# TensorE's order written out: attention steps between half chunks, the memory's scale moved to its evictions

## The chip, the cores and the metric

The kernel runs on one core of one Trainium2 chip. The metric is the device time of one execution in microseconds; the time before is 349.41 us, the median of 3 runs (348.76 to 350.09). Everything is computed in 32-bit floats: a projection product is made of three matmuls in the fp32r type (high part by high part, high by low, low by high), for which each weight and each activation is first split into a rounded high part and the remainder.

## The reference, cut to what matters

```
h = rmsnorm(x, norm_w);  proj = h @ w_in           # 256 tokens, 1024 -> 10752 columns
o_a = dilated_mixture(3 groups of q, k, v)          # 8 heads of 64, ALiBi
o_b = moba_attention(q, k, v)                       # 8 heads; 256 tokens: one causal block
kv  = rmsnorm(mem, mem_norm_w) @ w_mem_kv           # 256 memory tokens
o_m = memory_cross_attention(m_q, m_k, m_v)         # 4 heads
p_i = (o_i * silu(gate_i)) @ w_branch_i             # i = a, b, m
merged = sum_i sigmoid(logit_i + b_merge_i) * p_i
out = rmsnorm(x + merged @ w_out, final_norm_w)
```

## The kernel before, in words

All weights stream through as 54 chunks, listed by `_plan` in the order in which they are loaded, split and multiplied. A chunk is 128 x 2048 numbers: 256 columns of a projection with all 1024 rows, or an equal part of a branch or output matrix. Chunks 0 to 5 are q, k, v of branch b (two halves each), 6 to 10 the gates, 11 to 13 the memory's k and v and the query that reads it (Mk, Mv, Mq), 14 to 31 branch a (two halves of the heads, each with three dilation groups of q, k, v), 32 to 49 merge logits (L) and branch matrices (W), 50 to 53 the output matrix.

`load(i + 3)` puts a chunk's load on SP's queue. `split` has ScalarE cast the raw weights to the high part `wh` (3 buffers) and VectorE subtract it for the low part `wl` (2 buffers), in halves, two chunks ahead. TensorE then does 48 matmuls for the chunk, 24 for each half (`mm_feat` with the weights stationary, `mm_tok` with the activations stationary), into one of three PSUM banks `pj`. An eviction by ScalarE or VectorE follows: a gate chunk is read by a tanh and a product `g` (L633, L635), a query or key by `split_q` or `split_k`, which write fp32r high and low parts for the scores.

Attention runs beside the chunks. Each pair of heads is a list of steps: scores and softmax (`scores`: matmuls, then VectorE, ScalarE, VectorE), transposes of the weights through TensorE with a copy by ScalarE (`trans`), and the weighted values with the gate (`pv`). `chain` gives each step a slot, 2 x chunk + half; `pump` issues the steps that are due, between the two halves of a chunk or at its end. Slots of b start at chunk 12, those of m at chunk 16, those of a in the chunks behind each half of its heads. The scale of the memory's norm is computed by `mem_norm` (two squares on ScalarE, a power on POOL), spread over the partitions by one matmul with ones (`spread`) and multiplied into the memory in `mem_split`, ahead of the matmuls.

The order of the instructions on an engine is not the program's: a planner takes, by its own costs, the first instruction in the program's order that is ready when the engine comes free. So an attention step can run chunks earlier than its slot, and its matmuls can lie between those of a projection. Only for the last output chunk is TensorE's order the program's (`tc.manual_schedule`, L683). The order is fixed when the kernel is built; on the chip each engine goes through it and waits where something isn't ready.

Of the kernel before, what the change touches and what calls it, by code (L numbers as in the profile page):

```python
# [7 lines left out]
F32 = mybir.dt.float32  # L8
# [3 lines left out]
ALU = mybir.AluOpType  # L12
PSUM = bass.MemoryType.PSUM

P = 128
# [15 lines left out]
def _plan():  # L31

    out = []
    b0 = 5120
    for i, n in enumerate(ANAMES):
        for hf in range(2):
            out.append(("B" + n, hf, "in", b0 + 512 * i + (256 * hf if i else 0)))
    for hf in range(2):
        out.append(("G", ("b", hf), "in", 6656 + 256 * hf))
    for hf in range(2):  # L40
        out.append(("G", ("a", hf), "in", 4608 + 256 * hf))
    out.append(("G", ("m", 0), "in", 7424))
    out.append(("Mk", 0, "mem", 0))
    out.append(("Mv", 0, "mem", 256))
    out.append(("Mq", 0, "in", 7168))
    for hf in range(2):
        for g in range(3):
            for i, n in enumerate(ANAMES):
                out.append(("A" + n, (hf, g), "in", 1536 * g + 512 * i + 256 * hf))
    for br, off in (("b", 1), ("m", 2), ("a", 0)):  # L50
        for hf in range(2):
            for j in range(2):
                out.append(("L", (br, 2 * hf + j), "in", 7680 + 1024 * off + 256 * (2 * hf + j)))
            out.append(("W", (br, hf), br, 512 * hf))
    for j in range(4):
        out.append(("O", j, "out", 256 * j))
    return out
# [6 lines left out]
def kernel(ctx: ExitStack, tc: tile.TileContext, wts: bass.AP, xT_d: bass.AP, memT_d: bass.AP,  # L64
# [142 lines left out]
        nc.sync.dma_start(memst["T"], memT_d)  # L207

    def mem_norm():
        _, memst["dg"] = stats(memst["nat"], "m")  # L210

    def mem_split(lo, hi):
        if lo == 0:
            memst["h"] = cp.tile([P, KD, S], F32R, tag="xr", name="mh", bufs=2)
            memst["l"] = cp.tile([P, KD, S], F32R, tag="xr", name="ml", bufs=2)
        mt, mh, ml = memst["T"], memst["h"], memst["l"]
        for k in range(lo, hi):
            nc.vector.scalar_tensor_tensor(mt[:, k, :], mt[:, k, :], mnw[:, k:k + 1], rb["m"],
                                           op0=ALU.mult, op1=ALU.mult)
        for k in range(lo, hi, 2):  # L220
            nc.scalar.copy(mh[:, k:k + 2], mt[:, k:k + 2])
            nc.vector.tensor_tensor(ml[:, k:k + 2], mt[:, k:k + 2], mh[:, k:k + 2].bitcast(F32), op=ALU.subtract)


    def rtile(name):
# [318 lines left out]
                                       rb["x"][:, None, :].to_broadcast([P, 2, S]), op0=ALU.mult, op1=ALU.mult)  # L544


    for i, (kind, key, src, col) in enumerate(PLAN):
        if 0 < i < NCH - 3:
            load(i + 3)
        if i == 1:  # L550
# [15 lines left out]
        if i in (7, 11):  # L566
            hf = (i - 7) // 4
            qkv["Bkx", hf] = split_k(qkv["Bk", hf], f"Bk{hf}")
        if i == 7:
            mem_norm()  # L570
        if i in (9, 10):
            mem_split(4 * (i - 9), 4 * (i - 8))
        nat = kind[0] == "B"
        ah, al = (XH, XL) if nat else (HH, HL)
        if src == "mem":
# [2 lines left out]
        if kind in ("W", "O"):  # L578
            pass
        else:  # L580
            if i == 0:
                pss = [pa.tile([P, 512], F32, tag=("s", "pt")[f // 2], name=f"pj0{f}") for f in range(4)]
            elif i > 1:
                ps = pj.tile([P, 512], F32, tag="pj", name=f"pj{i}")
            if i < 2:
                mm_feat_outer(pss, i, XH, XL)
                split(i + 2, 2, 4)
                split(i + 2, 3, 4)
            for n in range(2 if i > 1 else 0):
                if tok:  # L590
                    mm_tok(ps, S * n, i, [a[:, P * n:P * (n + 1)] for a in ah], [a[:, P * n:P * (n + 1)] for a in al])
                else:
                    mm_feat(ps, S * n, i, KD, S, n, ah, al)
                if n == 0:
                    pump(i, 0)
                    if i == 3:
                        rb["x"] = spread(dgx, "x")
                    if i == 8:
                        rb["m"] = spread(memst["dg"], "m")
                    if i + 2 < NCH:  # L600
                        split(i + 2, 1, 2)
# [12 lines left out]
        elif kind in ("Aq", "Ak", "Av", "Mq", "Mk", "Mv"):  # L614
            at = (kind,) + (key if kind[0] == "A" else (0,))
            if kind[1] == "q" and at[-1] == 0:
                qkv[at] = split_q(ps, -SCALE, f"{kind}{i}")
            elif kind[1] == "k" and at[-1] == 0:
                qkv[at] = split_k(ps, f"{kind}{i}")
            elif kind == "Av" and key[1] > 0:  # L620

                hf, g = key
                if g == 1:
                    stacked[hf] = tp.tile([P, 2, 2, S], F32, tag="vs", name=f"vs{hf}")
                for r in range(2):
                    nc.scalar.copy(stacked[hf][64 * (g - 1):64 * g, :, r, :],
                                   ps[64 * r:64 * (r + 1)].rearrange("p (e c) -> p e c", e=2))
            else:
                t = qkv[at] = rtile(f"{kind}{i}")
                nc.scalar.mul(t, ps, -SCALE if kind == "Aq" else 1.0)  # L630
# [5 lines left out]
        elif kind == "L":  # L636
            br, bk = key
            th = ths[br, bk] = tp.tile([P, 512], F32, tag="th", name="thl")
            off = {"a": 0, "b": 8, "m": 16}[br]
            for n in range(2):  # L640
                c = off + 2 * bk + n
                nc.scalar.activation(th[:, S * n:S * (n + 1)], ps[:, S * n:S * (n + 1)], AF.Tanh, bias=hb[:, c:c + 1],
                                     scale=0.5)
        elif kind == "W":
            br, hf = key
            kn = 2 if br == "m" else 4
            oh = [og[br, k][0] for k in range(kn)]
            ol = [og[br, k][1] for k in range(kn)]
            if "t" not in acc:
                acc["t"] = cp.tile([P, 4, 512], F32, tag="xt", name="acc")  # L650
            for j in range(2):
                bk = 2 * hf + j
                ps = pj.tile([P, 512], F32, tag="pj", name=f"pw{i}{j}")
                for n in range(2):
                    mm_feat(ps, S * n, i, kn, 512, 2 * j + n, oh, ol)
                    if j == 1 and n == 0 and i + 2 < NCH:
                        split(i + 2, 1, 2)
                a = acc["t"][:, bk, :]
                if br == "b":
                    nc.vector.scalar_tensor_tensor(a, ths[br, bk], 1.0, ps, op0=ALU.add, op1=ALU.mult)  # L660
                else:
                    tmp = tp.tile([P, 512], F32, tag="mt", name="mt", bufs=1)
                    nc.vector.scalar_tensor_tensor(tmp, ths[br, bk], 1.0, ps, op0=ALU.add, op1=ALU.mult)
                    if br == "m":
                        nc.gpsimd.tensor_tensor(a, a, tmp, op=ALU.add)
                    else:
                        nc.vector.tensor_tensor(a, a, tmp, op=ALU.add)
                        mh = rp.tile([P, 2, S], F32R, tag="r", name=f"mgh{bk}")
                        ml = rp.tile([P, 2, S], F32R, tag="r", name=f"mgl{bk}")
                        nc.scalar.copy(mh.rearrange("p a b -> p (a b)"), a)  # L670
                        nc.vector.tensor_tensor(ml.rearrange("p a b -> p (a b)"), a,
                                                mh.rearrange("p a b -> p (a b)").bitcast(F32), op=ALU.subtract)
                        merged[bk] = (mh, ml)
                if j == 0:
                    pump(i, 0)
        else:
            if key < 2:
                order = [(key, i, 0), (key, i, 1)]
            elif key == 2:
                order = [(key, i, 0)]  # L680
            else:
                order = [(key, i, 0), (key - 1, i - 1, 1), (key, i, 1)]
            with tc.manual_schedule(engines={mybir.EngineType.PE}) if key == 3 else ExitStack():  # L683
                for kc, wi, t in order:
                    out_mm(kc, wi, t)
                    if t == 0 and i + 2 < NCH:
                        split(i + 2, 1, 2)
                    if kc == 3:
                        finish(t)
        if kind == "Bv" and key == 1:  # L690
            chain([pair_steps_b(p) for p in range(4)], 2 * i + 14, 2)
        elif kind == "Mq":
            chain([pair_steps_m(p) for p in range(2)], 2 * i + 6, 2)
        elif kind == "Av" and key[1] == 2:
            chain([pair_steps_a(2 * key[0] + p) for p in range(2)], 2 * i + 2, 4)
        pump(i, 1)
    assert not steps


# [63 lines left out]
```

## Time and profile before

| | |
|---|---|
| median of 3 runs | 349.41 us |
| profiled execution, its own time | 349.35 us |
| span of the profile | 347.6 us |
| TensorE matmuls busy | 338.2 us (97 %), 2924 |
| VectorE busy | 232.7 us (67 %) |
| ScalarE busy | 206.8 us (60 %) |
| mean granted TensorE clock | 0.994 |

The span runs from the first to the last instruction; the execution's own time holds 1.75 us more. A matmul's busy time contains its way through the array, and matmuls overlap, so what one costs is read from the distance between two starts and not from its duration. In the timeline, equal instructions in a row are merged: "x8" is eight of them, and the time beside it runs from the start of the first to the end of the last.

### The profile page before, as it was taken

Reading aid. Unit: us, or ns where it says so; the run is one execution under the profiler, and the core shown is the slowest. Engines: PE = TensorE matmul, PEld = TensorE weight load, DVE = VectorE, ACT = ScalarE, POOL = GpSimd, SP = SyncE. Lnnn points to the kernel's source line nnn. Section 1 sums busy time; section 2 is a strip of 40 time slices with the busy share of each in tenths; the row PEclk is TensorE's granted clock in tenths of the full one; section 3 lists DMA queues with packets and bytes.
Section 4 is the critical chain, followed back from the end, with each engine's and each line's share of the span. In section 5 each row is a group of like instructions: output and inputs, shape, how many; then the busy total and the mean of one; then the engine's idle time right before and its main releaser. Section 6 shows DMA issues by size and latency. Waiting matters only on the chain.

```text
span 347.6 us, 7107 instructions
## 1 busy us (share of the span) xinstructions
PE 338.2 (97%) x2924; PEld 323.6 (93%) x2924; DVE 232.7 (67%) x405; ACT 206.8 (60%) x367; POOL 27.1 (8%) x40
## 2 busy tenths in 40 slices
PE   8989999999999999999999999999999999999992
PEld 5989999999999988999999999999999999999882
DVE  3849999996878863537785444666453747667554
ACT  6767799575858664637856364765643465546322
POOL 2402000100001000000101000010000304000022
PEclk9999999999999999999999999999999999999997
DMA  7998788650475443354443436345235457646003
GB/s 205 317 413 329 252 352 269 238 210 19 143 275 183 138 173 123 121 219 145 128 163 133 186 130 234 124 158 191 75 123 181 135 232 241 243 138 226 0 3 122
DMA packets 12946, 63.33 MB, mean 182 GB/s; under 512 B 1393, under 2 KB 2801, under 8 KB 6641
## 3 DMA queue, kind: packets, MB, share of 16 engines
q1 hardware_dynamic: 12912, 62.88, 51.0%
q8 instruction: 23, 0.38, 0.4%
q14 instruction: 11, 0.08, 0.1%
HBM read 61.82 MB, written 1.05 MB: 181 GB/s over the span
## 4 chain that ended last, share of the span: by engine, by line
PE 90%; DMA 4%; DVE 2%; SPq 2%; ACT 1%; issue 1%; POOL 0%; POOLq 0%; DVEq 0%
PE pj L234 17%; PE pj L237 17%; PE pj L235 17%; PE pj L254 5%; PE pj L256 5%; PE pj L255 5%; PE pt L322 3%; PE pw L234 3%; PE pw L235 3%; PE pw L237 3%; DMA xn<-in_x 3%; PE y L494 2%; PE y L493 2%; PE y L495 2%; DMA wraw<-in_wts 2%; PE oa L389 1%
## 5 line engine op out<-in xcount | busy, mean ns | idle before, releaser
L94 DVE TENSOR_TENSOR wl<-wraw,wh 128x1024 fp32r<-128x1024 f32 (+2 forms) x117 | 129.7, 1145 | 65.7 <-issue 49.2
L93 ACT CAST wh<-wraw 128x1024 fp32r<-128x1024 f32 (+2 forms) x117 | 108.1, 968 | 49.5 <-PE pj L235 32.2
L234 PE MATMUL pj<-hh,wh 128*128 128x256 f32 x480 | 114.9, 281 | 0.7 <-DVE ssq_m L143 0.7
L235 PE MATMUL pj<-hl,wh 128*128 128x256 f32 x480 | 114.2, 279 | 0.2 <-DVE hl L199 0.2
L234 PEld LDWEIGHTS pj<-hh,wh 128*128 128x128 f32 x480 | 90.3, 188 | 1.8 <-PE sb L299 0.8
L235 PEld LDWEIGHTS pj<-hl,wh 128*128 128x128 f32 x480 | 90.4, 188 | 0.8 <-DVE hl L199 0.4
L237 PE MATMUL pj<-hh,wl 128*128 128x256 f32 x480 | 66.3, 279 | 0.0
L237 PEld LDWEIGHTS pj<-hh,wl 128*128 128x128 f32 x480 | 60.0, 188 | 0.0
L254 PE MATMUL pj<-wh,hh 128*128 128x256 f32 x96 | 27.0, 281 | 0.0
L256 PE MATMUL pj<-wh,hl 128*128 128x256 f32 x96 | 26.8, 279 | 0.0
L255 PE MATMUL pj<-wl,hh 128*128 128x256 f32 x96 | 26.6, 277 | 0.0
L314 ACT ACTIVATE u<-u,st 128x384 f32<-128x384 f32 (+2 forms) x32 | 16.9, 529 | 13.1 <-DVE st L308 13.1
L323 ACT COPY ptsb<-pt 128x384 f32<-128x384 f32 (+1 forms) x28 | 13.1, 497 | 10.4 <-PE pt L322 10.3
L254 PEld LDWEIGHTS pj<-wh,hh 128*128 128x128 f32 x96 | 18.0, 188 | 0.5 <-issue 0.4
L256 PEld LDWEIGHTS pj<-wh,hl 128*128 128x128 f32 x96 | 18.0, 188 | 0.4 <-issue 0.4
L255 PEld LDWEIGHTS pj<-wl,hh 128*128 128x128 f32 x96 | 18.0, 188 | 0.0
L356 POOL TENSOR_SCALAR nba<-con 128x512 f32<-128x512 f32 x8 | 5.0, 624 | 143.6 <-DVE st L308 143.2
L316 DVE TENSOR_SCALAR u<-u,st 128x256 f32<-128x256 f32 (+2 forms) x40 | 15.1, 398 | 0.6
L494 PE MATMUL y<-wl,mgh 128*128 128x512 f32 (+1 forms) x40 | 13.9, 348 | 0.0
L493 PE MATMUL y<-wh,mgh 128*128 128x512 f32 (+1 forms) x40 | 13.9, 347 | 0.0
L495 PE MATMUL y<-wh,mgl 128*128 128x512 f32 (+1 forms) x40 | 13.9, 346 | 0.0
L322 PE MATMUL pt<-con,u 128*128 128x128 f32 x88 | 13.0, 274 | 0.0
(195 smaller groups left out, 552.8 us busy)
## 6 DMA issues: line engine op xcount, KB each, us to landing
wraw<-in_wts SPq DMA_DIRECT2D x48, 1024.0 KB, 4.8
wraw<-in_wts SPq DMA_DIRECT2D x15, 256.0 KB, 5.7
xn<-in_x SPq DMA_DIRECT2D x1, 1024.0 KB, 9.0
memT<-in_memT SPq DMA_DIRECT2D x1, 1024.0 KB, 5.2
memn<-in_mem SPq DMA_DIRECT2D x1, 1024.0 KB, 8.0
xres<-in_xr SPq DMA_DIRECT2D x1, 1024.0 KB, 4.7
wraw<-in_wts SPq DMA_DIRECT2D x2, 512.0 KB, 3.2
out<-ysb SPq DMA_DIRECT2D x4, 256.0 KB, 2.0
```

The source lines that it names most:

```text
L93: nc.scalar.copy(whs[i][:, sl], raws[i][:, sl])
L94: lower[i] = nc.vector.tensor_tensor(wls[i][:, sl], raws[i][:, sl], whs[i][:, sl].bitcast(F32), op=ALU.subtract)
L234: nc.tensor.matmul(ps[:, lo:lo + S], wh[:, k, fs], ah[k], start=(k == 0), stop=False)
L235: nc.tensor.matmul(ps[:, lo:lo + S], wh[:, k, fs], al[k], start=False, stop=False)
L237: nc.tensor.matmul(ps[:, lo:lo + S], wl[:, k, fs], ah[k], start=False, stop=(k == kn - 1))
L254: nc.tensor.matmul(ps[:, lo:lo + S], ah[k], wh[:, k, :], start=(k == 0), stop=False)
L255: nc.tensor.matmul(ps[:, lo:lo + S], ah[k], wl[:, k, :], start=False, stop=False)
L256: nc.tensor.matmul(ps[:, lo:lo + S], al[k], wh[:, k, :], start=False, stop=(k == KD - 1))
L322: nc.tensor.transpose(ps[:, P * j:P * (j + 1)], u[:, P * c:P * (c + 1)], ident)
L493: nc.tensor.matmul(y[t, n][:, 0:w], ht, wh[:, k, cs], start=(kc == 0 and k == 0), stop=False)
L494: nc.tensor.matmul(y[t, n][:, 0:w], ht, wl[:, k, cs], start=False, stop=False)
L495: nc.tensor.matmul(y[t, n][:, 0:w], lt, wh[:, k, cs], start=False, stop=(kc == 3 and k == 1))
```

## The change

- From chunk 8 on all of the loop runs under `tc.manual_schedule` for TensorE: its instructions are issued as the program has them, each attention step where `pump` stands. The other engines are still planned. The separate order for the last output chunk is dropped, being included.
- The memory's query comes ahead of its keys and values (chunks 11, 12, 13 are now Mq, Mk, Mv). The norm of the memory moves from chunk 7 to 9, `mem_split` from chunks 9 and 10 to 10 and 11, the spread from chunk 8 to 11.
- `mem_split` no longer multiplies by the norm: ScalarE makes the high part from the memory and the norm's weight, VectorE the low part. The scale comes in at Mk's eviction (a product on VectorE, then the split) and at Mv's (ScalarE, by halves).
- Branch a takes its dilation groups in the order 1, 2, 0; its chain is started by the values of group 0. The slots of m start at chunk 18.

```diff
     out.append(("G", ("m", 0), "in", 7424))
+    out.append(("Mq", 0, "in", 7168))
     out.append(("Mk", 0, "mem", 0))
     out.append(("Mv", 0, "mem", 256))
-    out.append(("Mq", 0, "in", 7168))
     for hf in range(2):
-        for g in range(3):
+        for g in (1, 2, 0):
...
-        _, memst["dg"] = stats(memst["nat"], "m")
+        memst["r"], memst["dg"] = stats(memst["nat"], "m")
...
         for k in range(lo, hi):
-            nc.vector.scalar_tensor_tensor(mt[:, k, :], mt[:, k, :], mnw[:, k:k + 1], rb["m"],
-                                           op0=ALU.mult, op1=ALU.mult)
-        for k in range(lo, hi, 2):
-            nc.scalar.copy(mh[:, k:k + 2], mt[:, k:k + 2])
-            nc.vector.tensor_tensor(ml[:, k:k + 2], mt[:, k:k + 2], mh[:, k:k + 2].bitcast(F32), op=ALU.subtract)
+            nc.scalar.activation(mh[:, k, :], mt[:, k, :], AF.Copy, scale=mnw[:, k:k + 1])
+            nc.vector.scalar_tensor_tensor(ml[:, k, :], mt[:, k, :], mnw[:, k:k + 1], mh[:, k, :].bitcast(F32),
+                                           op0=ALU.mult, op1=ALU.subtract)
...
+    in_order = ctx.enter_context(ExitStack())
     for i, (kind, key, src, col) in enumerate(PLAN):
+        if i == 8:
+            in_order.enter_context(tc.manual_schedule(engines={mybir.EngineType.PE}))
...
-        if i == 7:
+        if i == 9:
             mem_norm()
-        if i in (9, 10):
-            mem_split(4 * (i - 9), 4 * (i - 8))
+        if i in (10, 11):
+            mem_split(4 * (i - 10), 4 * (i - 9))
...
-                    if i == 8:
+                    if i == 11:
                         rb["m"] = spread(memst["dg"], "m")
...
+            elif kind == "Mk":
+                t = rtile("Mk")
+                nc.vector.tensor_tensor(t.rearrange("p (f t) -> p f t", f=2), ps.rearrange("p (f t) -> p f t", f=2),
+                                        rb["m"][:, None, :].to_broadcast([P, 2, S]), op=ALU.mult)
+                qkv[at] = split_k(t, f"{kind}{i}")
+            elif kind == "Mv":
+                t = qkv[at] = rtile(f"{kind}{i}")
+                for n in range(2):
+                    nc.scalar.activation(t[:, S * n:S * (n + 1)], ps[:, S * n:S * (n + 1)], AF.Copy,
+                                         scale=memst["r"][:, n:n + 1])
...
-        elif kind == "Mq":
-            chain([pair_steps_m(p) for p in range(2)], 2 * i + 6, 2)
-        elif kind == "Av" and key[1] == 2:
+        elif kind == "Mv":
+            chain([pair_steps_m(p) for p in range(2)], 2 * i + 10, 2)
+        elif kind == "Av" and key[1] == 0:
             chain([pair_steps_a(2 * key[0] + p) for p in range(2)], 2 * i + 2, 4)
         pump(i, 1)
+    in_order.close()
```

## Rows read from the trace of the kernel before

**Rows 1.** The page, busy us (share of the span) xinstructions of TensorE.
```profile
PE 338.2 (97%) x2924; PEld 323.6 (93%) x2924; DVE 232.7 (67%) x405; ACT 206.8 (60%) x367; POOL 27.1 (8%) x40
```
**Rows 2.** Waits of TensorE: line, waited for, us in total, times, longest.
```profile
PE pj L234 <- DVE ssq_m L143: 0.7, 1, 0.7
```
**Rows 3.** Stretches: length, busy us of each engine (instructions), granted clock, DMA share, GB/s.
```profile
57.73:139.28 81.55, 80.83 (x668) 76.29 (x667) 64.56 (x155) 53.53 (x113) 4.51 (x9) 1.00 0.48 174
139.28:256.40 117.12, 117.12 (x1146) 113.57 (x1145) 68.92 (x115) 68.93 (x116) 3.73 (x6) 1.00 0.43 150
256.40:319.08 62.68, 62.68 (x556) 62.68 (x553) 37.77 (x40) 30.65 (x45) 7.01 (x4) 1.00 0.56 199
40.00:60.00 20.00, 19.09 (x166) 18.78 (x165) 19.75 (x28) 19.05 (x29) 0.49 (x1) 1.00 0.82 300
60.00:80.00 20.00, 20.00 (x167) 19.28 (x166) 20.00 (x62) 13.64 (x36) 2.38 (x7) 1.00 0.58 217
```
**Rows 4.** Timeline of TensorE: start us, us, line, out<-in xcount.
```profile
91.91 1.10 PE L237 MATMUL pj<-hh,wl 128*128 128x256 f32 x8
...
263.77 1.07 PE L237 MATMUL pj<-hh,wl 128*128 128x256 f32 x8
```
**Rows 5.** Timeline of TensorE around one unbroken attention block of b.
```profile
100.39 1.10 PE L237 MATMUL pj<-hh,wl 128*128 128x256 f32 x8
101.42 0.87 PE L429 MATMUL ob<-ptsb,Bv 128*64 128x256 f32 x8
102.22 0.87 PE L322 MATMUL pt<-con,u 128*128 128x128 f32 x6
102.85 0.36 PE L298 MATMUL sb<-Bk1y,Bq1x 128*128 128x256 f32 x1
...
103.80 0.33 PE L234 MATMUL pj<-hh,wh 128*128 128x256 f32 x1
103.97 0.28 PE L235 MATMUL pj<-hl,wh 128*128 128x256 f32 x1
```
**Rows 6.** Timeline of TensorE behind a single transpose between projections.
```profile
120.75 0.36 PE L235 MATMUL pj<-hl,wh 128*128 128x256 f32 x1
120.95 0.52 PE L237 MATMUL pj<-hh,wl 128*128 128x256 f32 x3
```
**Rows 7.** Timeline of TensorE from chunk 8's end to chunk 9's start.
```profile
57.73 0.28 PE L298 MATMUL sb<-Bk0y,Bq0x 128*128 128x256 f32 x1
...
58.50 0.27 PE L299 MATMUL sb<-Bk0z,Bq0x 128*128 128x128 f32 x1
59.49 0.36 PE L234 MATMUL pj<-hh,wh 128*128 128x256 f32 x1 [0.72 <-DVE ssq_m L143]
```
**Rows 8.** Timeline of VectorE at the same place.
```profile
58.67 0.68 DVE L635 SCALAR_TENSOR_TENSOR g<-thg,pj 128x512 f32<-128x512 f32 x1
```
**Rows 9.** Timeline of TensorE: a's scores end; values, then transposes of that softmax.
```profile
173.57 0.46 PE L370 MATMUL sa<-Ak,Aq 64*64 64x64 f32 x16
...
179.71 1.08 PE L389 MATMUL oa<-ptsb,Av 128*64 128x256 f32 x8
180.62 0.64 PE L396 MATMUL oa<-ptsb,vs 128*64 128x64 f32 x16
...
181.65 0.82 PE L322 MATMUL pt<-con,u 128*128 128x128 f32 x6
```
**Rows 10.** Groups of VectorE by form: busy us, mean ns, idle us before them.
```profile
L218 DVE SCALAR_TENSOR_TENSOR memT<-memT,small,rb_m 128x256 f32<-128x256 f32 x8 | 3.2, 476 | 0.0
L222 DVE TENSOR_TENSOR ml<-memT,mh 128x512 fp32r<-128x512 f32 x4 | 2.8, 718 | 0.0
```
**Rows 11.** Groups of ScalarE by form.
```profile
L153 ACT ACTIVATE xh<-xp 128x256 fp32r<-128x256 f32 x8 | 4.1, 507 | 0.9 <-DMA xp<-in_xT 0.8
```
**Rows 12.** Timeline of VectorE: last scaling of the b softmax behind [rows 5].
```profile
107.01 0.29 DVE L316 TENSOR_SCALAR u<-u,st 128x128 f32<-128x128 f32 x1
```
**Rows 13.** Timeline of VectorE: scaling of the a softmax behind [rows 9].
```profile
179.91 0.75 DVE L316 TENSOR_SCALAR u<-u,st 128x384 f32<-128x384 f32 x2
```

More of the change, by code (lines that the diff above doesn't have):

```diff
@@ L682 @@
                 order = [(key, i, 0), (key - 1, i - 1, 1), (key, i, 1)]
[L683 to L689, printed above, removed]
+            for kc, wi, t in order:
+                out_mm(kc, wi, t)
+                if t == 0 and i + 2 < NCH:
+                    split(i + 2, 1, 2)
+                if kc == 3:
+                    finish(t)
         if kind == "Bv" and key == 1:
             chain([pair_steps_b(p) for p in range(4)], 2 * i + 14, 2)
-        elif kind == "Mq":
-            chain([pair_steps_m(p) for p in range(2)], 2 * i + 6, 2)
-        elif kind == "Av" and key[1] == 2:
+        elif kind == "Mv":
+            chain([pair_steps_m(p) for p in range(2)], 2 * i + 10, 2)
+        elif kind == "Av" and key[1] == 0:
             chain([pair_steps_a(2 * key[0] + p) for p in range(2)], 2 * i + 2, 4)
         pump(i, 1)
+    in_order.close()
     assert not steps
```

## The prediction

> **What bounds the kernel now.** I read the busy times first, then TensorE's waits, then the stretches, and last the timeline of TensorE around the attention steps. The busy line [rows 1] has TensorE at 338.2 of 347.6 us; of its waits only one, of 0.7 us, lies where the change acts [rows 2]. By stretches [rows 3]: from 57.73 to 139.28 us (chunks 9 to 19 and the attention of branches b and m) and from there to 256.40 us (branch a) TensorE has no idle time to speak of. VectorE and ScalarE are full from 40 to 60 us (19.75 and 19.05 of 20.00 us), VectorE again from 60 to 80; over the whole first stretch VectorE has 17 of 81.55 us free, over the second 48 of 117.12. So TensorE sets the end, and what can be won is its time per instruction, not idle time. Three things make that time longer than it need be.
>
> First, its tempo. A projection matmul of 256 columns follows the one before by 113 ns in one state and by 117 to 118 in another: eight in a row take (1.07 - 0.28)/7 = 0.113 us at 263.77 and (1.10 - 0.28)/7 = 0.117 at 91.91 [rows 4]. The granted clock is 1.00 in both [rows 3], so it is not the clock. From 256.40 to 319.08 lie 552 projection matmuls and nothing else, 62.68/552 = 0.1135 us each [rows 3], so the short distance there, and before 57.73 too. Between them 400 of the 528 in the first stretch and 340 of 841 in the second follow at the long one, the first behind the step at 57.73, the last ahead of 249.29; they cost 740 x 4.6 ns = 3.4 us. The state changes at attention steps and at some chunk borders, and I found no rule in the trace that says which way.
>
> Second, going from projections to attention and back. In an unbroken block (weighted values, transposes, scores) eight matmuls take 0.80 us, six transposes 0.63, eight scores 0.95, the way in about 0.1 and the way back 0.06 [rows 5]: 2.53 us in all. Where the planner spliced single transposes between projections, one projection takes 0.20 us instead of 0.113 to 0.118 [rows 6]; some 20 such returns lie between 57.73 and 139.28.
>
> Third, the wait at chunk 9: TensorE has chunk 8 done at 57.73, does one score step of b, and then stands until 59.49 [rows 7]. Between the last two starts are 0.99 us instead of 0.11: 0.88 idle. It waits for the gate product g of chunk 6, which VectorE does at 58.67 [rows 8] and which frees the PSUM buffer that chunk 9 takes.
>
> **The change part by part.** Its own profiled execution took 349.35 us for a span of 347.6, so 1.75 us lie around the span; the median of the runs, 349.41, is 0.06 above it. The number of matmuls stays as it is.
>
> *Attention in unbroken blocks.* From 57.73 to 139.28 are 81.55 us. The 528 projection matmuls at 0.1134 make 59.85, the slower tempo 400 x 4.6 ns = 1.84, the idle part of the wait 0.88. Left are 18.98 us for attention, returns and the spread. In program order the steps come as ten blocks, one in the middle of each of chunks 12 to 21, priced from the whole block of [rows 5] and cut where a part is missing: scores of b alone 0.85 (their first costs less directly behind projections, as at 57.73 to 58.50 in [rows 7]); transposes and scores 1.58; two whole blocks 5.06; values and transposes 1.61; values alone 1.00. For m, scores are four narrow matmuls wider (0.95 alone, 1.03 behind transposes), eight transposes are 0.85 and values 0.91 (the first eight of oa, 179.71 to 180.62 in [rows 9]): 0.95, 1.88, 1.94 and 1.11. With 0.43 for the spread the sum is 16.4 us. If instead each of ten blocks paid 0.1 in and 0.1 out on top of the dearest parts, it would be 17.5. The gain is 1.5 to 2.6 us; I take 2.5, near the upper end, because the whole block is measured and two of the ten are that block. In branch a nearly every step is a block already and stands where the program has it, so I count nothing there; the one spliced step, scores around transposes at 181.19, would give some 0.05 us.
>
> The Trainium skill, "TensorE: Matmul & The Clock Gate", Part 2, says that weight loads are pulled ahead of matmuls in flight, so the next weights load while the current matmul runs. By that a change of operands would cost nothing and gathering the steps would gain nothing: the time would be 350.1 us. This trace speaks against it, with 0.20 us at a return [rows 6].
>
> *The wait at chunk 9.* In program order the b scores come in chunk 12, so nothing fills the time before 59.49. The idle time goes from 0.88 to 59.49 - 57.73 less one interval, 1.65 us: a loss of 0.8. The bounds are a gain of 0.9, if VectorE comes to g of chunk 6 before 57.7, and a loss of 2, if it comes a pair of weight splits (2.3 us) later. I take +0.8: the chunks ahead of 8 and VectorE's work for them are unchanged. What is queued behind the waiting matmul is all of TensorE, and VectorE's later work waits for that, but it has its own arrears until then.
>
> *The memory's scale.* VectorE loses 8 x 0.48 + 4 x 0.72 = 6.7 us of scaling and splitting and gets 8 x 0.48 = 3.8 back [rows 10], then one product of 128x512 at Mk's eviction (0.7 by the subtraction of that size). ScalarE gets 8 x 0.51 = 4.1 us [rows 11] for 4 copies of 0.6, and Mv's eviction in two halves, under 1 us more. All of it stands beside TensorE, which by program order reaches Mk only at chunk 12, about 59.5 + 3 x 5.5 + 0.4 = 76.4 us. With the softmax of b out of the time before that too, VectorE has less there than it had, so I cost it at nothing. If that cover went, its price is at most what VectorE lacks from 40 to 80 us, where it is full: 1 to 2 us before Mk. Mq ahead of Mk and Mv needs only h, which is ready. The spread matmul only moves; the two loads of the memory stay where they were on SP's queue, and POOL's one power operation moves two chunks back, with only bias products of b queued there, which then have until chunk 12.
>
> *The order of the a groups, 1, 2, 0.* It puts the splits of group 0's q and k in the last chunks before the a scores, which carry no attention. The k split (four casts and four subtractions, under 5 us) has the 8 us of chunk 22 and half of chunk 23: hidden. It takes the split out of a chunk with scores, where softmax was late by it (below). Weight loads follow the new order on SP's queue one for one; no queue gets more.
>
> *The new waits in program order.* A transpose step stands 48 matmuls (5.4 us), or 6.3 us where values go before it, behind its scores, and if softmax isn't done by then everything on TensorE waits. In the trace the b scores that end at 103.80 have their last scaling end at 107.30 [rows 12], after 3.5 us. But the a scores that end at about 174.0 have theirs at 180.66 [rows 9, 13], after 6.6 us, because VectorE put the k split ahead and two weight splits in between; the transposes only came at 181.65. From nothing to 1.2 us each; VectorE is lighter in chunks 13 to 16, so I take 0.
>
> *Tempo.* Between all fast and all slow the two stretches differ by 1369 x 4.6 ns = 6.3 us; before has 3.4 of it. I take no change.
>
> Sum: -2.5 + 0.8 + 0 = -1.7: 349.35 - 1.7 = 347.6 us.
>
> **The rivals.**
> - *The tempo or the wait helps as well.* Gathered blocks disturb TensorE less often, so most projections keep 113 ns (-1.5 or so), or g comes early (-0.9 instead of +0.8). For it: the long stretches without attention are all fast [rows 3, 4]. Against: blocks in branch a were followed by either state. 345 to 346.5 us.
> - *Late softmax eats the gain.* Two or three transpose steps wait 0.5 us each, or tempo worsens by 1 us: 348.5 to 349.5. For it: the 6.6 us above. Against: VectorE's 17 us of free time in the first stretch [rows 3], all of it after 80 us.
> - *Slower.* VectorE's order is fixed ahead by planned times; where it has k splits of Mk and weight splits ahead of softmax at chunks 12 to 16, program order has nothing to put in TensorE's gap, as the planner had. Six transpose steps of b and m and four places of memory work stand to lose; at 1 us each in five of them the balance is -1.7 + 5, 352.6. It decides from 1.7 us of such waits upward. For it: VectorE full up to 80 us, and the step that would be 1.2 us late. Against: the steps of branch a already run in program order without one wait [rows 2].
> - *Gathering isn't worth anything*: each of the returns is paid in the blocks as well, and only the 0.8 us at chunk 9 is left: 350.1 us. For it: the way into a block costs 0.1 us as well. Against: [rows 5] beside [rows 6].
>
> **How the numbers follow.** This kernel's measurements tell 0.5 % (1.75 us) from no change, so faster means under 347.66, slower over 351.16. The forecast, 346.8 to 348.4, has 0.43; more gain 0.22; gain eaten 0.17, gathering worth nothing 0.04; slower 0.14. Half of the forecast's share lies under 347.66: faster 0.22 + 0.22 = 0.44, same 0.21 + 0.17 + 0.04 = 0.42, slower 0.14. The range leaves out the deepest of the gains and most of the slower case: 345.1 to 350.8.
>
> **What would show it.** On TensorE after 57.73: no score step before chunk 12; one wait of about 1.6 us at chunk 9; blocks only in the middle of chunks, with projections between them unbroken; 16 to 17.5 us for the attention of b and m. VectorE's busy time falls by about 2 us, without effect. The prediction is wrong if TensorE's waits on ptsb's or softmax's makers add up to over 1 us, if there are waits for the memory's parts at chunk 12, or if the count of projections at 118 ns leaves 500 to 950.

## The result and the profile after

The changed kernel takes 352.59 us (median of 21 runs, 349.32 to 354.49), the kernel before 350.04 (21 runs, 348.76 to 352.88): a ratio of 1.0073, interval 1.0057 to 1.009. It is slower by 2.6 us where 1.7 us of gain were forecast, and outside the range of 345.1 to 350.8 us. The profiled execution took 352.46 us for a span of 350.6.

The busy line of the page after, beside [rows 1], and the granted clock of TensorE in 40 slices of the span:

```profile
PE 337.4 (96%) x2924; PEld 324.0 (92%) x2924; DVE 232.5 (66%) x402; ACT 208.6 (60%) x372; POOL 28.3 (8%) x40
...
PEclk9999998799999999999999999999999999999999
```

TensorE is as busy as before; what is new is a dip of the clock in the seventh and eighth slice (52.6 to 70.1 us). The waits of TensorE there (line, waited for, us in total, times, longest), beside the 0.7 of [rows 2]:

```profile
PE pj L232 <- DVE g L647: 3.4, 1, 3.4
...
PE pt L320 <- DVE u L314: 1.2, 2, 1.0
```

And its timeline from the last matmuls of chunk 8 over the start of chunk 9 to the place where the distance becomes normal again; it answers to [rows 7]:

```profile
56.06 1.07 PE L235 MATMUL pj<-hh,wl 128*128 128x256 f32 x8
60.51 0.55 PE L232 MATMUL pj<-hh,wh 128*128 128x256 f32 x1 [3.38 <-DVE g L647]
60.86 0.41 PE L233 MATMUL pj<-hl,wh 128*128 128x256 f32 x1
...
65.98 0.36 PE L233 MATMUL pj<-hl,wh 128*128 128x256 f32 x1
66.18 0.28 PE L232 MATMUL pj<-hh,wh 128*128 128x256 f32 x1
66.30 0.28 PE L233 MATMUL pj<-hl,wh 128*128 128x256 f32 x1
```

The last matmul of chunk 8 starts at 56.86 and the first of chunk 9 at 60.51: 3.65 us instead of 0.11, so 3.54 idle by the starts. (The profile's own figure for the same wait, in brackets in the timeline, is 3.38; it is counted from the modelled end of the matmul before. Below, waits at chunk 9 are by the starts, as in the prediction's 0.88 for the kernel before, unless the text says "by the waits".) Then 25 matmuls, from 60.86 to 66.18, follow each other by 5.32/25 = 0.213 us instead of 0.113: another 2.5 us. Stretches of 1 us (length, busy us of PE, PEld, DVE, ACT, POOL with instructions, granted clock, DMA share, GB/s) say why:

```profile
58.00:59.00 1.00, 0.00 (x0) 0.00 (x0) 0.97 (x3) 1.00 (x4) 0.00 (x0) 1.00 0.53 180
59.00:60.00 1.00, 0.00 (x0) 0.00 (x0) 0.97 (x2) 1.00 (x3) 0.00 (x0) 0.66 0.95 401
60.00:61.00 1.00, 0.49 (x2) 0.52 (x3) 0.97 (x2) 1.00 (x3) 0.00 (x0) 0.50 1.00 414
64.00:65.00 1.00, 1.00 (x7) 1.00 (x6) 1.00 (x3) 0.00 (x0) 0.00 (x0) 0.50 0.01 4
66.00:67.00 1.00, 1.00 (x10) 1.00 (x10) 0.00 (x0) 0.00 (x0) 0.00 (x0) 0.93 0.55 147
```

While TensorE stood, the granted clock fell from 1.00 to 0.50 (2.4 to 1.2 GHz), and it stayed there for more than five microseconds of full work. VectorE and ScalarE were busy all through the wait. Their timelines answer for the wait; VectorE first, where [rows 8] had g of chunk 6 at 58.67:

```profile
51.30 3.25 DVE L219 SCALAR_TENSOR_TENSOR ml<-memT,small,mh 128x256 fp32r<-128x256 f32 x8
54.47 2.36 DVE L94 TENSOR_TENSOR wl<-wraw,wh 128x1024 fp32r<-128x1024 f32 x2
56.86 1.39 DVE L272 SCALAR_TENSOR_TENSOR Bq1x<-Bq,Bq1x 64x512 fp32r<-64x512 f32 x2
58.26 0.68 DVE L289 TENSOR_TENSOR Bk1z<-Bk,Bk1y 64x512 fp32r<-64x512 f32 x1
...
59.67 0.69 DVE L647 SCALAR_TENSOR_TENSOR g<-thg,pj 128x512 f32<-128x512 f32 x1
```

ScalarE in the same stretch:

```profile
46.80 3.31 ACT L218 ACTIVATE mh<-memT,small 128x256 fp32r<-128x256 f32 x8
...
54.50 0.60 ACT L645 ACTIVATE thg<-pj 128x512 f32<-128x512 f32 x1
```

The kernel before did the memory's work on VectorE (L218 there) only after the spread, here:

```profile
68.35 3.25 DVE L218 SCALAR_TENSOR_TENSOR memT<-memT,small,rb_m 128x256 f32<-128x256 f32 x8
```

So the split of the memory runs 17 us earlier than its predecessor, in the stretch where both engines are full [rows 3], although the program has it one chunk later. Without the factor `rb["m"]` it waits only for the memory's load, the norm's weight and the buffers that the x parts leave behind chunk 5; the planner takes what is ready, and laid 3.3 us of it on each engine. The tanh of chunk 6 was done at 55.1, its product g came at 59.67: behind two weight splits, the two products of Bq1 and half of Bk1's split. Counted from the start of chunk 8's last matmul, g ended 1.73 us later before and 3.50 after. So of the longer wait, 0.88 is the score step that no longer stands in it, as predicted, and 1.78 is the late g.

From the end of chunk 8 to chunk 22, TensorE took 57.62 to 150.18 = 92.55 us before and 56.86 to 153.31 = 96.46 after, 3.91 more, taken apart by distances of starts: the wait at chunk 9 +2.66 (0.88 to 3.54), the slow clock +2.7 (the 25 matmuls and what lies at their edges), waits for softmax +1.2, the slow tempo -0.7 (395 projections to 236), attention, returns and spread -1.95 (19.04 to 17.09; e4 below, where the clock was full, has the same 17.09). From chunk 22 to the end it is 197.4 before and 197.3 after. Chunk 8 ended 0.8 earlier after. That is scatter of the start: all of it is there when chunk 3 begins (23.83 before, 23.06 after), ahead of all that the change touches, and the same kernel ended chunk 8 at 59.37 in another profile (e0 below).

The gathered blocks look as the prediction had them. A whole block after, beside [rows 5]:

```profile
104.53 1.07 PE L235 MATMUL pj<-hh,wl 128*128 128x256 f32 x8
105.53 0.87 PE L427 MATMUL ob<-ptsb,Bv 128*64 128x256 f32 x8
106.33 0.87 PE L320 MATMUL pt<-con,u 128*128 128x128 f32 x6
106.96 0.36 PE L296 MATMUL sb<-Bk1y,Bq1x 128*128 128x256 f32 x1
...
107.91 0.34 PE L232 MATMUL pj<-hh,wh 128*128 128x256 f32 x1
```

From 105.53 to 107.91 it takes 2.38 us, with values, transposes and scores at 0.80, 0.63 and 0.95 as before.

### The profile page after: what moved, and what is told of

The parts are those of the page before. It is cut to its first block, busy times and chain, and to the rows that moved or that the text cites. A ratio compares the mean times of both kernels' runs of the same rounds, so it can differ in the third digit from the quotient of the medians.

```text
span 350.6 us, 7110 instructions
## 1 busy us (share of the span) xinstructions
PE 337.4 (96%) x2924; PEld 324.0 (92%) x2924; DVE 232.5 (66%) x402; ACT 208.6 (60%) x372; POOL 28.3 (8%) x40
## 4 chain that ended last, share of the span: by engine, by line
PE 84%; DVE 6%; DMA 5%; ACT 2%; issue 1%; SPq 1%; POOL 0%; POOLq 0%; DVEq 0%
PE pj L232 16%; PE pj L235 16%; PE pj L233 16%; PE pj L252 4%; PE pj L254 4%; PE pj L253 4%; PE pt L320 3%; PE pw L232 3%; PE pw L233 3%; PE pw L235 3%; DMA wraw<-in_wts 3%; DMA xn<-in_x 2%; PE y L492 2%; PE y L491 2%; PE y L493 2%; DVE wl L94 2%
## 5 line engine op out<-in xcount | busy, mean ns | idle before, releaser
L232 PE MATMUL pj<-hh,wh 128*128 128x256 f32 x480 | 116.3, 284 | 3.4 <-DVE g L647 3.4
L232 PEld LDWEIGHTS pj<-hh,wh 128*128 128x128 f32 x480 | 91.6, 191 | 4.5 <-issue 4.1
L233 PEld LDWEIGHTS pj<-hl,wh 128*128 128x128 f32 x480 | 91.6, 191 | 0.4 <-DVE hl L199 0.4
```

The costliest lines, as they stand in the source:

```text
L232: nc.tensor.matmul(ps[:, lo:lo + S], wh[:, k, fs], ah[k], start=(k == 0), stop=False)
L233: nc.tensor.matmul(ps[:, lo:lo + S], wh[:, k, fs], al[k], start=False, stop=False)
```

## The experiments

Theory A: the memory's split, freed of the scale, runs early and delays g; the idle time that follows also costs the clock. Theory B: TensorE's written order is at fault, because it leaves the gap unfilled and makes softmax a wait. Ratios are to the kernel before on the same chip (its medians were 349.65 for e1 to e4, 349.63 for the others); each kernel has 5 to 12 executions.

**e1: the scale goes back.** Order, chunks and blocks stay as changed.

```diff
-            nc.scalar.activation(mh[:, k, :], mt[:, k, :], AF.Copy, scale=mnw[:, k:k + 1])
-            nc.vector.scalar_tensor_tensor(ml[:, k, :], mt[:, k, :], mnw[:, k:k + 1], ...)
+            nc.vector.scalar_tensor_tensor(mt[:, k, :], mt[:, k, :], mnw[:, k:k + 1], rb["m"], ...)
...   casts and subtractions as before; mem_norm at chunk 8, spread at 9; Mk and Mv evicted unscaled
```

> The changed kernel with only the memory's scale put back into mem_split (norm at chunk 8, spread in chunk 9, evictions of Mk and Mv as before); TensorE in program order, chunk order as changed. Theory A (freed of the scale, mem_split was planned into VectorE's and ScalarE's full time at 47 to 54 us and put off the gate product g of chunk 6): mem_split goes back behind the spread, g comes at about 58.7, the wait at chunk 9 is 1.5 to 2 us, the granted clock stays at 1.00 behind it, and the time is 1.0 to 1.5 % under the changed kernel, 347.5 to 349. Theory B (the order alone is at fault, nothing fills the gap): wait over 3 us and the fall of the clock stay, 352 to 353.

Measured: 349.78 us (348.99 to 350.96), ratio 1.0005 (0.999 to 1.002). Its wait at chunk 9:

```profile
PE pj L234 <- DVE ssq_m L143: 1.6, 1, 1.6
```

By the starts it is 1.75 us, beside the 1.65 of the prediction. (The line names ssq_m, a small product that VectorE ends just after g. Chunk 9 starts 0.15 us after g's end here and after the change, and 0.14 before, so it's g that it waits for.) The granted clock stays at 1.00, and the stretch to chunk 22 is 92.40. The place and the price are A's; the time lies a little above what A expected, and the profile still has three softmax waits (1.0 together) and one for the spread (0.3).

**e2: matmuls in the gap.** 24 matmuls whose output nobody reads are added between chunks 8 and 9.

```diff
+            if i == 9:
+                pf = pa.tile([P, 512], F32, tag="o", name="fill", bufs=1)
+                for _ in range(24):
+                    nc.tensor.matmul(pf[:, 0:S], HH[0][:, 0:P], HH[0], start=True, stop=True)
```

> The changed kernel with 24 matmuls whose result nobody reads, put between chunks 8 and 9 on TensorE. They wait for nothing, so they lie in the wait for g (2.7 of its 3.5 us). If the low clock behind the wait is a cost of its own: clock 1.00 from 60 to 66 us, chunk 9 starts as late as before, and the time falls by the 2.6 us that the 27 slow matmuls cost, to about 350. If what follows is bound by VectorE anyway and the low clock hides in that: no change, 352 to 353.

Measured: 351.3 us (350.82 to 353.53), ratio 1.0054 (1.0033 to 1.0076). The added matmuls fill the whole gap: chunk 9 starts at 61.94, 3.12 us after chunk 8's last matmul (3.65 after the change), and at a granted clock of 1.00:

```profile
62.00:63.00 1.00, 1.00 (x9) 1.00 (x10) 0.99 (x2) 1.00 (x2) 0.00 (x0) 1.00 0.86 344
```

The stretch to chunk 22 is 93.26, 3.2 less than after: 2.7 for the clock (2.6 expected) and 0.5 for the shorter gap. The median is only 1.3 less, and the intervals of the two ratios overlap, so the medians alone don't show it. The mean granted clock, which is on record for every execution, does more. After the change, 18 of 21 executions have 0.988 to 0.993, with a median of 353.0 us; the other three have 0.996 or 0.997 and took 349.32, 350.97 and 351.76. The kernel before has 0.995 or more in all 48 executions beside these runs, and e2 in seven of eight, with 350.82 to 351.75 us. So the clock is lost in most executions and not in all, and by these times losing it costs about 2 us, as far as three executions without the loss can tell.

**e3: the memory's split held.** It may only be issued behind the tanh and the product of chunk 8; nothing else is touched.

```diff
         if i in (10, 11):
-            mem_split(4 * (i - 10), 4 * (i - 9))
+            with tc.issue_after(gated_at[8][0]), tc.issue_after(gated_at[8][1]):
+                mem_split(4 * (i - 10), 4 * (i - 9))
```

> The changed kernel, with mem_split's instructions on ScalarE and VectorE queued behind the tanh and the gate product of chunk 8; the work is the same. Theory A: as in the kernel with the scale put back, g of chunk 6 at about 58.7, wait 1.5 to 2 us, clock 1.00, 347.5 to 349. If instead it is the new form of the split (8 small casts for 4 large) that costs: 352 to 353.

Measured: 349.40 us (348.45 to 350.82), ratio 0.999 (0.9974 to 1.0006). Waits, and the clock at the place of the gap:

```profile
PE pj L232 <- DVE ssq_m L143: 1.6, 1, 1.6
PE pt L320 <- DVE u L314: 1.2, 2, 1.0
```

```profile
59.00:60.00 1.00, 0.50 (x4) 0.53 (x5) 1.00 (x4) 1.00 (x2) 0.48 (x1) 1.00 1.01 418
60.00:61.00 1.00, 1.00 (x11) 1.00 (x11) 1.00 (x2) 1.00 (x3) 0.23 (x1) 1.00 0.95 332
```

The smallest edit takes back some 3 us and gives the predicted wait; the expectation had not counted the 1.2 us for softmax. With e1 this settles A for the late g and the slow clock: two ways of keeping the memory's split out of 46 to 55 us give the same wait of 1.6 (1.75 by the starts) and no slow clock. It doesn't clear the order: the wait for softmax is still there, and e5 tells what the order adds.

**e4: everything early held.** As e3, and the splits of Bq1 and Bk1 and the memory's norm are held behind the tanh and the product of chunk 7.

```diff
-            qkv["Bqx", hf] = split_q(qkv["Bq", hf], 1.0, f"Bq{hf}")
+            with ExitStack() as held:
+                if hf:
+                    for ins in gated_at[7]:
+                        held.enter_context(tc.issue_after(ins))
+                qkv["Bqx", hf] = split_q(qkv["Bq", hf], 1.0, f"Bq{hf}")
...   the same for split_k of Bk1 and for mem_norm
```

> As the kernel that holds mem_split, and the splits of Bq1 and Bk1 and the memory's norm queued behind the tanh and the gate product of chunk 7 as well. Theory A carried on: g of chunk 6 comes before TensorE ends chunk 8, the wait at chunk 9 goes altogether (another 1.6 us), 345.5 to 347.5, under both kernels. Rival: the splits are then late for the b scores, or VectorE's arrears show up as another wait before chunk 12: 348 to 350.

Measured: 347.28 us (346.79 to 349.01), ratio 0.9937 (0.9915 to 0.9959). Chunk 9 follows chunk 8 without a pause (57.73 to 57.84). VectorE shows how: g comes first, Bq1 and Bk1 later.

```profile
52.19 0.68 DVE L658 SCALAR_TENSOR_TENSOR g<-thg,pj 128x512 f32<-128x512 f32 x1
...
55.77 1.41 DVE L272 SCALAR_TENSOR_TENSOR Bq1x<-Bq,Bq1x 64x512 fp32r<-64x512 f32 x2
...
60.88 0.68 DVE L289 TENSOR_TENSOR Bk1z<-Bk,Bk1y 64x512 fp32r<-64x512 f32 x1
```

The wait for softmax is left, at chunk 14. TensorE, and then VectorE between the scores (ended 85.27) and their last scaling:

```profile
90.97 0.87 PE L427 MATMUL ob<-ptsb,Bv 128*64 128x256 f32 x8
92.84 0.98 PE L320 MATMUL pt<-con,u 128*128 128x128 f32 x6 [1.00 <-DVE u L314]
```

```profile
85.70 0.29 DVE L306 CUSTOM_DVE_ANT_0 u<-sb,nbb 128x128 f32<-128x128 f32 x1
...
85.91 0.68 DVE L289 TENSOR_TENSOR Mk12z<-Mk,Mk12y 64x512 fp32r<-64x512 f32 x1
86.61 0.79 DVE L290 TENSOR_TENSOR Mk12z<-Mk,Mk12y 64x512 fp32r<-64x512 f32 x1
...
89.71 1.21 DVE L94 TENSOR_TENSOR wl<-wraw,wh 128x1024 fp32r<-128x1024 f32 x1
...
92.16 0.99 DVE L314 TENSOR_SCALAR u<-u,st 128x256 f32<-128x256 f32 x4
```

Mk's split and weight splits stand between the parts of softmax, which takes 7.9 us instead of the 3.5 of [rows 12].

**e0: the changed kernel once more**, beside e5 to e7.

> The changed kernel as it is, on the chip of the other runs of this group, so that they are compared on one chip: 352 to 353 us, the wait of 3.4 us at chunk 9 and the low clock behind it in the profile.

Measured: 352.67 us (351.65 to 354.44), ratio 1.0094 (1.0071 to 1.0118). Its wait at chunk 9:

```profile
PE pj L232 <- DVE g L647: 2.8, 1, 2.8
```

By the starts it is 3.0; then come 14 matmuls at 0.212 us (62.84 to 65.81), 1.4 us more. So the size of both varies from profile to profile of one kernel. So does the tempo: this profile has 336 slow projections up to chunk 22 where the profile after had 236.

**e5: the planner's order back.** All of the change but the written order (which stays for the last chunk alone).

```diff
-        if i == 8:
+        if i == NCH - 1:
             in_order.enter_context(tc.manual_schedule(engines={mybir.EngineType.PE}))
```

> The changed kernel without the order: TensorE planned as before up to the last chunk, everything else as changed. Theory A (the scale's early split puts off g of chunk 6): the split lies at 47 to 54 us as in the changed kernel and g comes at about 59.7; TensorE puts one score step (0.8 us) into the wait, some 2.7 us stay idle; 350 to 352.5, depending on whether the clock falls. If program order alone were at fault: as before, 349.5.

Measured: 350.43 us (349.14 to 352.39), ratio 1.0022 (1.0004 to 1.0039). The score step goes into the gap again, and still TensorE waits for g, which VectorE now does at 59.92:

```profile
57.76 0.28 PE L296 MATMUL sb<-Bk0y,Bq0x 128*128 128x256 f32 x1
...
58.53 0.27 PE L297 MATMUL sb<-Bk0z,Bq0x 128*128 128x128 f32 x1
60.76 0.36 PE L232 MATMUL pj<-hh,wh 128*128 128x256 f32 x1 [1.96 <-DVE g L646]
```

```profile
60.00:61.00 1.00, 0.24 (x2) 0.27 (x3) 0.97 (x2) 1.00 (x2) 0.00 (x0) 1.00 0.97 410
61.00:62.00 1.00, 1.00 (x11) 1.00 (x11) 0.99 (x2) 1.00 (x2) 0.00 (x0) 0.97 0.99 303
62.00:63.00 1.00, 1.00 (x7) 1.00 (x6) 0.97 (x8) 1.00 (x3) 0.14 (x1) 0.50 1.00 381
```

So the late g isn't the order's doing; the order makes the idle time 0.9 to 1.4 us longer (3.0 and 3.5 against 2.1 by the starts), by the score step that filled it. The clock fell here too, at about 62, after TensorE had already worked for 1.2 us: 15 matmuls from 61.99 to 65.19 at 0.213, 1.5 us. The executions agree with that price: the six with a mean clock of 0.990 to 0.993 took 350.37 to 351.29 us, the three with 0.995 or more 349.14 to 349.52.

Two more things stand in this trace. TensorE never waits for softmax, so the 1.2 us after the change is the written order's, as theory B has it. And attention, returns and spread take 17.58 us up to chunk 22, with 16 ways back to projections behind chunk 9's start instead of 22 before and 11 after, counting the spread's: of the 1.95 us saved, 1.46 come with the rest of the change, under the planner's order, and only 0.5 with the written one. On one chip the written order, with the split early, costs 352.67 - 350.43 = 2.2 us.

**e6: Mk's split later.** As e4, with the split of Mk moved from the end of chunk 12 to the start of chunk 16, behind the b softmaxes that it stood among.

```diff
+        if i == 16:
+            qkv["Mk", 0] = split_k(qkv["Mkn"], "Mk")
...
-                qkv[at] = split_k(t, f"{kind}{i}")
+                qkv["Mkn"] = t
```

> As the kernel that holds all of the splits (347.28 us), with the split of Mk moved from chunk 12's end to chunk 16's start. If the 1.0 us that the transposes in chunk 14 wait comes from Mk's four casts and four subtractions ahead of the exponentials: the wait goes, 346.0 to 346.8. If it comes from the weight splits between the softmax's parts: it stays, 347.3.

Measured: 345.93 us (344.95 to 346.46), ratio 0.989 (0.9872 to 0.9908): faster than both kernels. What is left of the wait at the transposes, and the step at chunk 14 (which the 1.00 preceded in e4):

```profile
PE pt L320 <- DVE u L314: 0.2, 1, 0.2
```

```profile
91.02 0.87 PE L427 MATMUL ob<-ptsb,Bv 128*64 128x256 f32 x8
91.82 0.87 PE L320 MATMUL pt<-con,u 128*128 128x128 f32 x6
```

**e7: the kernel before, with the same holding.** No other part of the change: Bq1, Bk1 and the norm held behind chunk 7's tanh and product.

> The kernel before (planned order, scale in mem_split, old chunk order) with the splits of Bq1 and Bk1 and the memory's norm queued behind the tanh and the gate product of chunk 7. Tells what of the 347.28 us is owed to the holding alone. If only the idle 0.9 us at chunk 9 goes: 348.3 to 349. If the holding alone does it, program order being worth nothing: 347.3. If the spread of the memory's scale is now late and stops mem_split: over 350.

Measured: 349.02 us (348.05 to 351.21), ratio 0.998 (0.9962 to 0.9997). The wait is gone here too and the stretch to chunk 22 is 90.83, but the median gains only 0.6 us. The holding alone is therefore not what makes e4 fast: with the rest of the change it is 347.28, 1.7 us less. The stretch to chunk 22 shows 0.7 of that: attention, returns and spread 18.85 us in e7 and 17.09 in e4, tempo 0.1, less the 1.2 us that e4 waits for softmax. The other 1.0 lies ahead of it, where chunk 8 ended at 58.78 in e7 and 57.73 in e4: 0.4 is there when chunk 3 begins, and 0.6 is added by the end of chunk 8, where e7 runs at the slow tempo (5.65 us for a chunk where e4 mostly has 5.44). One profile of each doesn't say whether that is more than scatter.

Not tested is the planner's order with the splits held and the rest of the change in place. e5 has 0.5 us more than e4 for attention and returns but none of the 1.2 for softmax, so nothing here shows that e4 or e6 owe their gain to the written order.

## Why the prediction was wrong, step by step

- **The step that failed** is the wait at chunk 9: "I take +0.8: the chunks ahead of 8 and VectorE's work for them are unchanged." The list of VectorE's work was unchanged, but not its order. The memory's split was priced by its length and by where the program has it, "All of it stands beside TensorE", "so I cost it at nothing"; that the edit also took away the one input that had kept it until after the spread was not seen, though the prediction names the spread and the planner takes whatever is ready. Measured: +2.66 for the wait where +0.8 was predicted (bounds -0.9 to +2). The +0.8 itself came, as 0.88 for the missing score step; the other 1.78 is the late g. Once the split is out of the way, e1 and e3 give 1.75 us of idle time where 1.65 was predicted.
- **Its second half** was no term at all: a longer wait costs the clock. In the trace of before the clock was 1.00 in every stretch that was read, and the prediction had no price for losing it. Measured: 2.5 to 2.7 us after, 1.4 in e0, 1.5 in e5. The Trainium skill, "TensorE: Matmul & The Clock Gate", Part 1 ("HAM oscillation"), describes the mechanism: the engine idles for a transfer, falls to the low clock, and pays half of the time spent there. This case agrees: from 60.51 to 66.18 at 0.50 that would be 2.8 us, and 2.7 are found; but what it waited for was VectorE.
- **Attention in blocks**: -2.5 predicted (1.5 to 2.6), -1.95 measured. Right in size, inside its bounds, and the blocks look as forecast; but the prediction put all of it down to program order, and e5 has three quarters of it without. Which of the other parts of the change brings that wasn't tested; the later slots of m are the obvious one. The Trainium skill, same page, Part 2, by which weight loads pulled ahead would have made this nothing, as the prediction read it, isn't borne out as to the sum: e4 against e7 shows 1.8 us of it with the clock full in both.
- **Softmax**: 0 predicted (nothing to 1.2 us each), 1.2 measured, nearly all of it at one step, and over the 1 us that the prediction named as a sign of being wrong; e5 shows that it comes with the written order. The slower rival's mechanism ("k splits of Mk and weight splits ahead of softmax at chunks 12 to 16") is real, as e4 and e6 show, but at one place and not five, under the 1.7 us from which it decides (that much takes away the gain; for a time over 351.16, the prediction's own bound, the sum needs 3.5). That its 352.6 us is nearly the time measured is chance.
- **Tempo**: 0 predicted, -0.7 measured in the profile after, but only -0.3 in e0, the same kernel. 228 to 254 slow projections instead of 395 are found in e4, e6 and e7 alike, and e7 has the old order. Ahead of 57.73 nearly all projections are fast in the trace of before, as the prediction says; e7 runs all of chunks 4 to 8 at the slow tempo. What sets the state stays open.
- **The rest**: the a order at nothing is right as far as seen (197.4 and 197.3 us from chunk 22 on). For Mk TensorE had no wait at chunk 12. VectorE's memory work fell by 2.0 us as forecast (6.0 to 4.0), but its whole busy time only from 232.7 to 232.5.

In sum: predicted -2.5 + 0.8 = -1.7; in the profiles -1.95 + 2.66 + 2.7 + 1.2 - 0.7 = +3.9 from the end of chunk 8 on, of which the scatter of the start hid 0.8, so that the two profiled executions differ by 3.1; the medians differ by 2.55.

## What to carry to other kernels

An edit that takes an input away from planned work can move that work to wherever it first becomes ready: look at when its remaining inputs land and what the engine has there, not at the line of the program. Where a buffer's release decides when TensorE goes on, hold early but unhurried work behind the releasing instruction; here that turned +2.6 us into -2.4, and one more delayed split into -3.7. And price a wait of TensorE together with the clock behind it.

## What the runs showed of the hardware

The granted clock fell from 1.00 to 0.50 after an idle time of 3.5 us (after; it fell while TensorE still stood), of 3.0 (e0; as work began again) and of 2.1 (e5; 1.2 us after work had begun again), and stayed at 0.50 for 3 to 6 us of full work. After 1.75 us, in e1 and e3, it didn't fall, nor in three of 21 executions after the change, going by their mean clock. At 0.50 a 256-column fp32r matmul followed the one before by 0.213 us, against 0.113. So one wait of a few microseconds near the edge of VectorE's capacity costs up to 1.8 times its length (2.7 on 3.54), and not the same in every execution.
